# One more unit of seven products in each down-projection, its sums of weights made and split during the up-projection

## The chip, the cores and the metric

The kernel runs on one core of a Trainium2 chip. The metric is the device time of one execution in microseconds (us). The engines are named as the profile names them: PE multiplies matrices, DVE and ACT work on vectors, POOL is a slower vector engine, SP issues the large transfers.

## The reference, cut to what matters

A trunk of two decoder layers for 256 tokens of 1024 features, in float32. Each layer is an attention and a feed-forward; a final RMSNorm closes. With 256 tokens, layer 0's block-sparse attention is plain causal attention over 16 heads. Layer 1 is sliding-window attention (window 128, 4 shared key/value heads, a learned sink for each head). The feed-forward is what the change touches:

```python
def conv_ffn(h, w_up, conv_w, conv_b, w_down):
    S_ = h.shape[1]
    u = h @ w_up
    up = jnp.pad(u, ((0, 0), (CONV_W - 1, 0), (0, 0)))
    u = conv_b + sum(conv_w[j] * up[:, j:j + S_] for j in range(CONV_W))
    gate, val = jnp.split(u, 2, axis=-1)
    return (jax.nn.silu(gate) * val) @ w_down
...
    x = x + conv_ffn(rmsnorm(x, ffn_norm[l]), w_up[l], conv_w[l], conv_b[l], w_down[l])
```

`w_up` is 1024 x 5632 (2816 gate and 2816 value columns), `w_down` is 2816 x 1024, the convolution has width 3.

## The kernel before, in words

**Three products for one.** Every matrix product is made of three passes of PE in a reduced float32 format. Each operand is split into a hi part (the value rounded to that format) and a lo part (value minus hi); PE adds hi x hi, hi x lo and lo x hi. For weights, ACT makes the hi part (L216, `hi_part`, tile `wh`) and DVE the lo part (L227, `lo_part`, tile `wl`). So each weight costs PE time, an ACT pass and a DVE pass.

**Units.** Weights come in units of 128 x 2048 float32 (1 MB), fetched by SP (`fetch`, L180) into three raw buffers (`wr`), in the order in which they are used, and split into rings of four `wh` and four `wl` buffers. `prepare(i)` plans the fetching and splitting of unit i, and is called by `used(i - 4)` when the unit four before it has been put on PE. Steps are queued by `chain(key, (delay, function), ...)` against a planned clock that `tick` moves on with each matmul; `require(key)` issues what is left of a chain at once, because its result is now needed. `w_time` is the planned time of the next split: 4500 ns behind the last, 2500 behind a unit of sums.

**The order of the work.** Python's order of issue is the order on PE, ACT, DVE and SP until attention A starts; from there (`manual.close()`) a scheduler orders the instructions of each engine from that program. Within an engine instructions run in their order, so one that waits holds up all behind it.

**Feed-forward** (`ffn`, L771). First the up-projection: 22 units, each giving 128 gate and 128 value columns with 48 matmuls of 256 tokens. `post` (L810) does the convolution (ACT L827, DVE L831 and L833), the gate (ACT L837) and the product of gate and value (POOL L838, tile `m` or `q`). The result is hidden block i; two blocks make hidden pair i, the input of down unit i. For a normal down unit each block's hi part comes from ACT (L846) and its lo part from DVE (L847). These values live in `qd`, a ring of 15 buffers called quads (tile `q`), each of 128 x 1024.

Then the down-projection, class `Down`: 11 units, each 256 rows of `w_down`, added up in four PSUM banks `acc` (two blocks of tokens by two halves of the columns). A normal unit takes 8 products of 128 x 128 by 128 x 512, times three passes: 24 matmuls (L641, L642, L644).

**Units of seven.** A unit can do the same 2 x 2 block product with 7 products instead of 8, if sums and differences of blocks are made on both sides (`seventh`, L650; matmuls L668 to L670): 21 matmuls. The table `SEVEN` names them: units 3, 5 and 7 in layer 0; 3, 5, 7 and 8 in layer 1. What is added on the weights' side: four sums of 128 x 512 (`sums_of`, L193; DVE L199 makes two, L203 one each) in two quads, and their split, as a unit of its own of the `wh`/`wl` rings (a unit of sums, name `wl<-sums,wh`). The unit itself then needs only three of its four column blocks. On the side of the activations: four differences by POOL (`mix`, L854), then a hi part by ACT (L862) and a lo part by DVE (L866) of the whole 128 x 1024 pair (`split`, L856), in two quads; the raw quad is then free. Four products of each unit of seven go to extra PSUM banks, which `gather` (L675) adds at the end.

**Around it.** `v_sb` holds the values of attention A, and later, in the same tiles, those of attention B and a mask `near` for it, made by POOL behind attention A (L1109 to L1113). `kd` are two tiles of keys with zeros in their off-diagonal blocks (L944), used in the scores of both attentions.

## Time and profile before

| | |
|---|---|
| median of 3 runs | 542.82 us (542.77 to 543.08) |
| profiled execution | 542.62 us, span 540.9 us |
| granted clock of PE | 0.997 |
| moved by DMA | 100.99 MB, 187 GB/s over the span |

The span is the time from the first to the last instruction that the profile shows; 1.7 us of the profiled execution lie around it. All times in the views count from the span's start. In the timeline a row has a start, a length, the engine, the line, what is written and read, and how many instructions the row joins; in brackets stands the idle time ahead of it and what ended it. Instructions of an engine overlap a little in these rows (a matmul of 512 columns is shown as 0.38 us, while the next starts 0.22 behind it), so the distance between starts is the pace. Up-projection 0 runs to about 230.5 us and its down-projection to 285; in layer 1 to about 480 and 534.5.

### The profile page before, as it was taken

The numbers are of one execution on the slowest core, as the hardware profiler recorded it, in microseconds if no ns is written. First come the engines' busy times: TensorE is split into PE (matmuls) and PEld (weight loads), VectorE is DVE, ScalarE is ACT, GpSimd is POOL, SyncE is SP. The second block draws the span as 40 slices with busy tenths as digits, with TensorE's granted clock in tenths as the row PEclk, the third lists the DMA queues.
The fourth block names the chain that finished last, engine by engine and source line by source line (L and its number), as shares of the span: only waits on it lengthen the run. The fifth ranks groups of instructions, "written<-read, shape, count | busy, mean of one in ns | idle before, by whom it ended". The sixth has DMA issues, their size and how long they took to land.

```text
span 540.9 us, 9984 instructions
## 1 busy us (share of the span) xinstructions
PE 533.2 (99%) x3721; PEld 490.2 (91%) x3721; DVE 460.9 (85%) x911; ACT 385.7 (71%) x741; POOL 155.5 (29%) x196
## 2 busy tenths in 40 slices
PE   9999999999999999999999999999999999999995
PEld 7888888899999999988888887789999999998884
DVE  6798868689888978899889788889899789799995
ACT  6989776679566776656568798787657766676744
POOL 8322002011424434251010166202434344420004
PEclk9999999999999999999999999999999999999998
DMA  8974545342456656644664544233466466654502
GB/s 315 399 261 170 194 156 167 147 146 90 156 233 234 224 179 221 234 156 157 233 233 164 225 156 156 80 125 110 157 237 228 170 223 234 231 197 157 202 33 78
DMA packets 16608, 100.99 MB, mean 187 GB/s; under 512 B 1968, under 2 KB 2352, under 8 KB 6064
## 3 DMA queue, kind: packets, MB, share of 16 engines
q1 hardware_dynamic: 16272, 100.22, 51.3%
q8 instruction: 29, 0.48, 0.4%
q10 hardware_dynamic: 288, 0.13, 0.1%
q14 instruction: 19, 0.16, 0.1%
HBM read 99.30 MB, written 1.05 MB: 186 GB/s over the span
## 4 chain that ended last, share of the span: by engine, by line
PE 92%; ACT 4%; DVE 3%; issue 1%; POOL 0%; DVEq 0%; ACTq 0%
PE u L791 7%; PE u L792 7%; PE u L790 7%; PE acc L644 6%; PE acc L641 6%; PE acc L642 6%; PE t L792 6%; PE t L790 6%; PE t L791 6%; PE acc L399 5%; PE acc L401 5%; PE acc L400 5%; ACT m L522 2%; PE acc L933 2%; PE acc L792 2%; PE acc L791 2%
## 5 line engine op out<-in xcount | busy, mean ns | idle before, releaser
L227 DVE TENSOR_TENSOR wl<-wr,wh 128x1024 fp32r<-128x1024 f32 (+1 forms) x186 | 200.3, 1093 | 20.2 <-ACT wh L216 19.8
L216 ACT ACTIVATE wh<-wr 128x1024 fp32r<-128x1024 f32 (+1 forms) x190 | 174.0, 942 | 25.0 <-PE acc L644 8.1
L790 PE MATMUL u<-q,wh 128*128 128x256 f32 x320 | 88.3, 277 | 0.0
L791 PE MATMUL u<-q,wh 128*128 128x256 f32 x320 | 88.2, 276 | 0.1
L792 PE MATMUL u<-q,wl 128*128 128x256 f32 x320 | 87.9, 275 | 0.0
L838 POOL TENSOR_TENSOR m<-m,m 128x256 f32<-128x256 f32 x30 | 50.0, 1667 | 113.3 <-DVE m L833 66.0
L790 PE MATMUL t<-q,wh 128*128 128x256 f32 x288 | 79.2, 275 | 0.0
L791 PE MATMUL t<-q,wh 128*128 128x256 f32 x288 | 79.2, 275 | 0.0
L792 PE MATMUL t<-q,wl 128*128 128x256 f32 x288 | 79.2, 275 | 0.0
L641 PE MATMUL acc<-wh,q 128*128 128x512 f32 x182 | 71.0, 390 | 0.2 <-ACT q L599 0.2
L642 PE MATMUL acc<-wl,q 128*128 128x512 f32 x182 | 69.4, 381 | 0.0
L791 PEld LDWEIGHTS u<-q,wh 128*128 128x128 f32 x320 | 61.4, 192 | 0.3 <-DVE q L363 0.3
L792 PEld LDWEIGHTS u<-q,wl 128*128 128x128 f32 x320 | 61.4, 192 | 0.0
L790 PEld LDWEIGHTS u<-q,wh 128*128 128x128 f32 x320 | 61.3, 192 | 0.0
L644 PE MATMUL acc<-wh,q 128*128 128x512 f32 x182 | 58.2, 381 | 0.0
L790 PEld LDWEIGHTS t<-q,wh 128*128 128x128 f32 x288 | 55.3, 192 | 0.0
L791 PEld LDWEIGHTS t<-q,wh 128*128 128x128 f32 x288 | 55.3, 192 | 0.0
L792 PEld LDWEIGHTS t<-q,wl 128*128 128x128 f32 x288 | 55.3, 192 | 0.0
L399 PE MATMUL acc<-wh,q 128*128 128x512 f32 x128 | 50.0, 391 | 0.0
L400 PE MATMUL acc<-wl,q 128*128 128x512 f32 x128 | 48.8, 381 | 0.0
L401 PE MATMUL acc<-wh,q 128*128 128x512 f32 x128 | 48.6, 380 | 0.0
L641 PEld LDWEIGHTS acc<-wh,q 128*128 128x128 f32 x182 | 34.4, 189 | 5.5 <-ACT q L599 0.6
(218 smaller groups left out, 1174.1 us busy)
## 6 DMA issues: line engine op xcount, KB each, us to landing
wr<-in_w SPq DMA_DIRECT2D x82, 1024.0 KB, 4.8
wr<-in_w SPq DMA_DIRECT2D x16, 512.0 KB, 6.4
first<-in_xw SPq DMA_DIRECT2D x7, 384.0 KB, 6.4
xr<-in_x SPq DMA_DIRECT2D x2, 512.0 KB, 8.3
fin_t<-in_fin SPq DMA_DIRECT2D x1, 512.0 KB, 6.5
out<-ot SPq DMA_DIRECT2D x1, 512.0 KB, 2.6
first<-in_xw SPq DMA_DIRECT2D x1, 388.0 KB, 3.5
out<-yo SPq DMA_DIRECT2D x1, 256.0 KB, 2.1
```

Of the source, the lines that this page charges most:

```text
L216: nc.scalar.activation(wq[i][0][:, c], raw_of(i, c), AF.Copy, **({} if g is None else {"scale": g}))
L227: nc.vector.tensor_tensor(out=lo, in0=raw, in1=hi, op=ALU.subtract)
L399: nc.tensor.matmul(o, xh[:, blk(b)], wh, start=(c == 0), stop=False)
L400: nc.tensor.matmul(o, xh[:, blk(b)], wl, start=False, stop=False)
L401: nc.tensor.matmul(o, xl[:, blk(b)], wh, start=False, stop=(c == KC - 1))
L641: nc.tensor.matmul(o, ph[:, blk(b)], turns(hi[:, s_]), start=first, stop=False)
L642: nc.tensor.matmul(o, ph[:, blk(b)], turns(lo[:, s_]), start=False, stop=False)
L644: nc.tensor.matmul(o, pl[:, blk(b)], turns(hi[:, s_]), start=False, stop=end)
L790: nc.tensor.matmul(o, hi[:, s_], xh, start=(c == 0), stop=False)
L791: nc.tensor.matmul(o, hi[:, s_], xl, start=False, stop=False)
L792: nc.tensor.matmul(o, lo[:, s_], xh, start=False, stop=(c == KC - 1))
L838: nc.gpsimd.tensor_tensor(out=h, in0=gs, in1=t[1], op=ALU.mult)
```

## The change

Down unit 4 becomes a unit of seven too, in both layers (`SEVEN`). Its sums of weights (`MADE`) aren't made in the down-projection and take no place in the rings of `wh` and `wl`:

- A copy of unit 4's weights is fetched once more, into the raw ring ahead of up unit 12 (`AHEAD`). While the up-projection runs, `make` forms the four sums in place with four DVE additions of 128 x 512 (L231 of the new file) and splits them: hi by ACT (L234) into two tiles `made` that use the memory of `v_sb`, lo by DVE (L237) into the two `kd` tiles. The raw buffer is handed on to the next fetch only after that. `w_time` is moved by 4500 ns for it.
- In the down-projection unit 4 is fetched and split in three of its four blocks (`SHORT`: 1536 columns, split in 1024 and 512). `seventh` takes its sums from `made` and `kd`.
- Its hidden pair is handled like the other pairs of seven: product on POOL, `mix`, then `split` with a start 3500 ns ahead of its base time instead of 6500.
- In layer 0, `again` runs 4000 ns (planned) after unit 4: it allocates `v_sb` once more, makes `near` (which no longer happens behind attention A) and writes the zeros of `kd` by two ACT instructions of 128 x 1024. In layer 1 it isn't needed.

PE has 3 matmuls fewer in each layer.

```diff
@@ -51,25 +51,32 @@
-SEVEN = ((3, 5, 7), (3, 5, 7, 8))
-U_KV = U_DN0 + NF // 2 + len(SEVEN[0])
+SEVEN = ((3, 4, 5, 7), (3, 4, 5, 7, 8))
+MADE = (4, 4)
+RING = tuple(tuple(k for k in SEVEN[l_] if k != MADE[l_]) for l_ in range(2))
+U_KV = U_DN0 + NF // 2 + len(RING[0])
 U_QB = U_KV + 2
 U_OB = U_QB + 4
 U_UP1 = U_OB + 4
 U_DN1 = U_UP1 + NF
-N_UNITS = U_DN1 + NF // 2 + len(SEVEN[1])
+N_UNITS = U_DN1 + NF // 2 + len(RING[1])
 def slot(layer, i):
-    return (U_DN0, U_DN1)[layer] + i + sum(k < i for k in SEVEN[layer])
-SUMS = [slot(l_, i_) + 1 for l_ in range(2) for i_ in SEVEN[l_]]
-RAW = {}
+    return (U_DN0, U_DN1)[layer] + i + sum(k < i for k in RING[layer])
+SUMS = [slot(l_, i_) + 1 for l_ in range(2) for i_ in RING[l_]]
+SHORT = [slot(l_, MADE[l_]) for l_ in range(2)]
+AHEAD = 12
+RAW, WIDX = {}, {}
 for k_ in range(N_UNITS):
+    for l_ in range(2):
+        if k_ == (U_UP0, U_UP1)[l_] + AHEAD:
+            RAW["made", l_] = len(RAW)
     if k_ not in SUMS:
-        RAW[k_] = len(RAW)
-NEXT = {k_: min((j_ for j_ in RAW if RAW[j_] == n_ + 3), default=N_UNITS) for k_, n_ in RAW.items()}
+        RAW[k_], WIDX[k_] = len(RAW), len(WIDX)
+NEXT = {k_: next((j_ for j_ in RAW if RAW[j_] == n_ + 3), None) for k_, n_ in RAW.items()}
@@ -178,10 +185,12 @@
     def fetch(i):
-        if i < N_UNITS and i not in SUMS:
-            raws[i] = wp.tile([P, UNIT], F32, tag="raw", name=f"wr{i}", bufs=3)
-            for c in (slice(0, UNIT // 2), slice(UNIT // 2, UNIT)) if 2 <= i < 10 else (slice(0, UNIT),):
-                nc.sync.dma_start(raws[i][:, c], w[RAW[i]][:, c])
+        if i in RAW:
+            of = SHORT[i[1]] if isinstance(i, tuple) else i
+            raws[i] = wp.tile([P, UNIT], F32, tag="raw", name=nm("wr"), bufs=3)
+            for c in ((slice(0, UNIT // 2), slice(UNIT // 2, UNIT)) if 2 <= of < 10 else
+                      (slice(0, 3 * UNIT // 4 if i in SHORT else UNIT),)):
+                nc.sync.dma_start(raws[i][:, c], w[WIDX[of]][:, c])
@@ -203,6 +212,33 @@
         chain(("t", i), (500.0, both), (900.0, lambda: more(2, 0, 2)), (600.0, lambda: more(3, 2, 1)))
+    made_hi = []
+    def made_parts(k, part):
+        at = (0, 3, 2, 1)[k]
+        return (made_hi, made_lo)[part][at // 2][:, half(at % 2)]
+    def make(layer):
+        key = ("made", layer)
+        made_hi[:] = [one.tile([P, D], F32R, tag=f"v{b}", name=nm("made")) for b in range(NB)]
+        raw = raws[key]
+        s_ = [raw[:, half(k)] for k in range(4)]
+        def add(to, a, b):
+            nc.vector.tensor_tensor(out=s_[to], in0=s_[a], in1=s_[b], op=ALU.add)
+        def hi(n):
+            nc.scalar.activation(made_hi[n], raw[:, n * D:(n + 1) * D], AF.Copy)
+        def lo(n):
+            nc.vector.tensor_tensor(out=made_lo[n], in0=raw[:, n * D:(n + 1) * D], in1=f(made_hi[n]), op=ALU.subtract)
+        chain(key, (600.0, lambda: add(0, 0, 3)), (600.0, lambda: add(3, 2, 3)), (600.0, lambda: add(2, 0, 2)),
+              (600.0, lambda: add(1, 2, 1)), (600.0, lambda: hi(0)), (1000.0, lambda: hi(1)), (200.0, lambda: lo(0)),
+              (1000.0, lambda: lo(1)), (100.0, lambda: fetch(NEXT[key])))
@@ -260,8 +296,12 @@
                 sums_of(i + 2)
-        if i + 1 in SUMS:
+            for l_ in range(2):
+                if i + 1 == (U_UP0, U_UP1)[l_] + AHEAD:
+                    w_time[0] += 4500.0
+                    make(l_)
+        if i + 1 in SUMS or i in SHORT:
             cut[1] = slice(UNIT // 2, 3 * UNIT // 4)
...
@@ -650,25 +689,32 @@
             u = self.at(i)
+            made = i == MADE[self.layer]
             need(u)
-            need(u + 1)
+            if made:
+                require("made", self.layer)
+            else:
+                need(u + 1)
             self.wait(i)
             if not self.more:
                 self.more = [bank(t) for t in ("u", "t", "u", "t")]
             one, five, six, sev = self.more
-            (rh, rl), (th, tl) = wq[u], wq[u + 1]
+            def right(k, sum_, part):
+                return made_parts(k, part) if sum_ and made else wq[u + sum_][part][:, half(k)]
             xh, xl = self.parts[2 * i]
             (a00, a01), (a10, _) = self.acc
             own = dict(start=i == SEVEN[self.layer][0], stop=i == SEVEN[self.layer][-1])
-            for o, x_, hi, lo, k, mine in ((one, 0, rh, rl, 0, True), (six, 6, th, tl, 2, True), (five, 5, th, tl, 0, True),
-                                           (sev, 4, th, tl, 1, True), (a00, 2, rh, rl, 1, False), (a01, 7, rh, rl, 2, False),
-                                           (a10, 3, th, tl, 3, False)):
-                o, wh, wl = pairs(o), turns(hi[:, half(k)]), turns(lo[:, half(k)])
+            for o, x_, sum_, k, mine in ((one, 0, 0, 0, True), (six, 6, 1, 2, True), (five, 5, 1, 0, True), (sev, 4, 1, 1, True),
+                                         (a00, 2, 0, 1, False), (a01, 7, 0, 2, False), (a10, 3, 1, 3, False)):
+                o, wh, wl = pairs(o), turns(right(k, sum_, 0)), turns(right(k, sum_, 1))
                 c = blk(x_)
                 nc.tensor.matmul(o, xh[:, c], wh, start=mine and own["start"], stop=False)
                 nc.tensor.matmul(o, xh[:, c], wl, start=False, stop=False)
                 nc.tensor.matmul(o, xl[:, c], wh, start=False, stop=mine and own["stop"])
                 tick(3 * 512 / 2.4)
+            if made and self.layer == 0:
+                chain(("again",), (4000.0, again))
             if own["stop"]:
@@ -693,7 +739,8 @@
                     used(self.at(i))
-                    used(self.at(i) + 1)
+                    if i != MADE[self.layer]:
+                        used(self.at(i) + 1)
                     yield 21 * 512 / 2.4
@@ -862,7 +909,7 @@
             parts[2 * i] = tuple(t.rearrange("p c t -> p (c t)") for t in (hi, lo))
-            chain(("a", i), (5000.0 * (i - 2) + (300.0 if i == 3 else -6500.0), high),
+            chain(("a", i), (5000.0 * (i - 2) + (300.0 if i == 3 else -3500.0 if i == 4 else -6500.0), high),
                   (800.0, lambda: nc.vector.tensor_tensor(out=lo, in0=raw, in1=f(hi), op=ALU.subtract)))
...
@@ -1106,11 +1154,19 @@
-    near = v_sb[0][:, NKV:NKV + 4].rearrange("p h d -> p (h d)").rearrange("p (k t) -> p k t", k=2)
-    nc.gpsimd.memset(near, 1.0)
-    for k, (op, sign) in enumerate(((ALU.is_gt, 1), (ALU.is_ge, -1))):
-        nc.gpsimd.affine_select(out=near[:, k], in_=near[:, k], compare_op=op, fill=0.0, base=0,
-                                pattern=[[-sign, P]], channel_multiplier=sign)
+    near = []
+    def again():
+        v_sb[:] = [one.tile([P, NH, HD], F32, tag=f"v{b}", name=nm("v")) for b in range(NB)]
+        near.append(v_sb[0][:, NKV:NKV + 4].rearrange("p h d -> p (h d)").rearrange("p (k t) -> p k t", k=2))
+        nc.gpsimd.memset(near[0], 1.0)
+        for k, (op, sign) in enumerate(((ALU.is_gt, 1), (ALU.is_ge, -1))):
+            nc.gpsimd.affine_select(out=near[0][:, k], in_=near[0][:, k], compare_op=op, fill=0.0, base=0,
+                                    pattern=[[-sign, P]], channel_multiplier=sign)
+        for t in kd:
+            nc.scalar.activation(t.rearrange("p a b t -> p (a b t)").rearrange("p (k t) -> p k t", t=P),
+                                 ones.unsqueeze(1).to_broadcast([P, 8, P]), AF.Copy, scale=0.0)
...
```

Where the order of instructions moves, three places (rows are line, operation, output, inputs, shape; the numbers in the names of tiles tell buffers apart and differ between the two programs).

The first is the start of layer 0's down-projection, on DVE. Before: lo part of pair 3, first half of unit 3's sums, a block's lo part (L847), lo part of pair 5, second half of unit 3's sums, a block's lo part.

```order
L866 TENSOR_TENSOR q_3000<-q_1854,q_2999 128x1024
L227 TENSOR_TENSOR wl_3059<-sums_2989,wh_3058 128x1024
L847 TENSOR_TENSOR q_2853<-m_284_2924,q_2853 128x256
L866 TENSOR_TENSOR q_3002<-q_2142,q_3001 128x1024
L227 TENSOR_TENSOR wl_3059<-sums_2990,wh_3058 128x1024
L847 TENSOR_TENSOR q_2853<-m_291_2998,q_2853 128x256
```

The same place now (L913 is the lo part of a pair, L263 of weights, L894 of a block); the L913 rows are pairs 3, 4 and 5.

```order
L913 TENSOR_TENSOR q_3007<-q_1851,q_3006 128x1024
L263 TENSOR_TENSOR wl_3068<-sums_2996,wh_3067 128x1024
L894 TENSOR_TENSOR q_2860<-m_328_2931,q_2860 128x256
L913 TENSOR_TENSOR q_3009<-q_1993,q_3008 128x1024
L263 TENSOR_TENSOR wl_3068<-sums_2997,wh_3067 128x1024
L913 TENSOR_TENSOR q_3011<-q_2141,q_3010 128x1024
L894 TENSOR_TENSOR q_2860<-m_336_3005,q_2860 128x256
```

The lo part of pair 4 has the place that pair 5 had, and pair 5 comes behind the second half of unit 3's sums.

On ACT at the same place, before: hi parts of unit 3's sums, with that of pair 5 (L862) between them, then of a block (L846) and of unit 4's weights.

```order
L216 ACTIVATE wh_3058<-sums_2989 128x1024
L862 ACTIVATE q_3001<-q_2142 128x1024
L216 ACTIVATE wh_3058<-sums_2990 128x1024
L846 ACTIVATE q_2853<-m_291_2998 128x256
L216 ACTIVATE wh_3093<-wr_2910 128x1024 x2
```

And now (L909 is the hi part of a pair, L893 of a block, L252 of weights):

```order
L252 ACTIVATE wh_3067<-sums_2996 128x1024
L252 ACTIVATE wh_3067<-sums_2997 128x1024
L893 ACTIVATE q_2860<-m_336_3005 128x256
L909 ACTIVATE q_3010<-q_2141 128x1024
L252 ACTIVATE wh_3104<-wr_2917 128x1024
L252 ACTIVATE wh_3104<-wr_2917 128x512
L909 ACTIVATE q_3012<-q_2430 128x1024
```

The hi part of pair 5 now stands behind that of the block, which reads what POOL's product wrote; the one of pair 4 went ahead of these rows.

The second place is layer 1's down-projection on DVE, between units 3 and 6. Before: pairs 5, 7 and 8 are the L866 rows, with the sums of unit 5 (L199, L203) and the weights of units 4 and 5 between them.

```order
L866 TENSOR_TENSOR q_6003<-q_5144,q_6002 128x1024
L847 TENSOR_TENSOR q_5853<-m_569_5998,q_5853 128x256
L199 TENSOR_TENSOR sums_6134<-wr_5981 128x1024
L227 TENSOR_TENSOR wl_6097<-wr_5910,wh_6096 128x1024 x2
L203 TENSOR_TENSOR sums_6135<-sums_6134,wr_5981 128x512
L203 TENSOR_TENSOR sums_6135<-sums_6135,wr_5981 128x512
L866 TENSOR_TENSOR q_6005<-q_5428,q_6004 128x1024
L227 TENSOR_TENSOR wl_6131<-wr_5981,wh_6130 128x1024
L227 TENSOR_TENSOR wl_6131<-wr_5981,wh_6130 128x512
L866 TENSOR_TENSOR q_6007<-q_5569,q_6006 128x1024
L227 TENSOR_TENSOR wl_6171<-sums_6134,wh_6170 128x1024
```

Now the L913 rows are pairs 5 and 7; pair 8 follows three rows below the last one.

```order
L913 TENSOR_TENSOR q_6030<-q_5161,q_6029 128x1024
L263 TENSOR_TENSOR wl_6126<-wr_5935,wh_6125 128x1024
L263 TENSOR_TENSOR wl_6126<-wr_5935,wh_6125 128x512
L208 TENSOR_TENSOR sums_6163<-wr_6006 128x1024
L212 TENSOR_TENSOR sums_6164<-sums_6163,wr_6006 128x512
L212 TENSOR_TENSOR sums_6164<-sums_6164,wr_6006 128x512
L263 TENSOR_TENSOR wl_6160<-wr_6006,wh_6159 128x1024
L263 TENSOR_TENSOR wl_6160<-wr_6006,wh_6159 128x512
L913 TENSOR_TENSOR q_6032<-q_5450,q_6031 128x1024
L263 TENSOR_TENSOR wl_6197<-sums_6163,wh_6196 128x1024
```

Unit 4's lo part is shorter by half a row, the sums of unit 5 come after it and not around it, and pair 7 stands behind the weights of unit 5.

The third place is a little later in layer 1, on DVE: the sums of unit 8 and their lo parts. Before:

```order
L227 TENSOR_TENSOR wl_6249<-sums_6223,wh_6248 128x1024
L199 TENSOR_TENSOR sums_6275<-wr_6162 128x1024
L227 TENSOR_TENSOR wl_6268<-wr_6162,wh_6267 128x512
L203 TENSOR_TENSOR sums_6276<-sums_6275,wr_6162 128x512
L203 TENSOR_TENSOR sums_6276<-sums_6276,wr_6162 128x512
L227 TENSOR_TENSOR wl_6302<-sums_6275,wh_6301 128x1024
L227 TENSOR_TENSOR wl_6302<-sums_6276,wh_6301 128x1024
```

And now (L208 and L212 are the additions, L263 the lo parts):

```order
L263 TENSOR_TENSOR wl_6284<-sums_6249,wh_6283 128x1024
L208 TENSOR_TENSOR sums_6301<-wr_6191 128x1024
L263 TENSOR_TENSOR wl_6299<-wr_6191,wh_6298 128x512
L212 TENSOR_TENSOR sums_6302<-sums_6301,wr_6191 128x512
L263 TENSOR_TENSOR wl_6328<-sums_6301,wh_6327 128x1024
L212 TENSOR_TENSOR sums_6302<-sums_6302,wr_6191 128x512
L263 TENSOR_TENSOR wl_6328<-sums_6302,wh_6327 128x1024
```

The last addition stood ahead of both lo parts; now it stands between them.

More of the change, by code (lines that the diff above doesn't have):

```diff
@@ L320, in trunk @@
     for b in range(NB):
-        t = one.tile([P, NH, HD], F32, name=f"v{b}")
-        v_sb.append(t)
+        v_sb.append(one.tile([P, NH, HD], F32, tag=f"v{b}", name=nm("v")))
     def warm_up(n):
@@ L553, in part @@
                 nc.vector.tensor_tensor(out=pT[:, :, 1:], in0=tp[:, :, 1:].to_broadcast(shape),
-                                        in1=near.unsqueeze(1).to_broadcast(shape), op=ALU.mult)
+                                        in1=near[0].unsqueeze(1).to_broadcast(shape), op=ALU.mult)
             chain(("pT", j), (200.0, lambda: nc.scalar.activation(pT[:, :, 0], tp[:, :, 0], AF.Copy)), (100.0, part))
@@ L946, in trunk @@
         nc.gpsimd.memset(f(t), 0.0)
+    made_lo = [t.rearrange("p a b t -> p (a b t)") for t in kd]
     invf = rb[:, 144:152]
@@ L1298, in pack @@
     rows2(inp["w_down"][1], SEVEN[1])
-    assert len(units) == len(RAW)
+    assert len(units) == len(WIDX)
     wpk = np.stack(units)
```

## The prediction

> **What bounds the kernel.** I read the head of the page first: busy time by engine, as a share of the span.
>
> ```profile
> span 540.9 us, 9984 instructions
> PE 533.2 (99%) x3721; PEld 490.2 (91%) x3721; DVE 460.9 (85%) x911; ACT 385.7 (71%) x741; POOL 155.5 (29%) x196
> ```
>
> The matmuls fill 99% of the span. The waits of PE show whether anything holds it up now (engine, line, what it waited for, total, times, longest):
>
> ```profile
> PE u L329 <- DVE warm L304: 1.1, 1, 1.1
> PE u L547 <- ACT m L532: 0.2, 1, 0.2
> PE acc L641 <- ACT q L599: 0.2, 1, 0.2
> ```
>
> No wait of PE lies in a feed-forward. A matmul taken out is time taken out, as long as its operands still come in time. Who makes them is the next question: the windows of the two down-projections (busy time of each engine with its count, then the granted clock, the DMA share and GB/s).
>
> ```profile
> core 0: us, PE busy (x) PEld busy (x) DVE busy (x) ACT busy (x) POOL busy (x), PEclk, DMA share, GB/s
> 230.50:284.50 54.00, 54.00 (x257) 47.09 (x255) 49.22 (x65) 33.13 (x47) 12.71 (x12) 1.00 0.53 195
> 480.40:534.50 54.10, 54.10 (x257) 47.50 (x257) 50.25 (x63) 34.09 (x46) 8.97 (x6) 1.00 0.35 127
> ```
>
> PE is full, but DVE, which makes the lo parts and the sums, is at 49.2 and 50.3 of 54 us. The change takes work from PE in this stage and must not bring DVE's results later. So the case is decided by the lead of each split over its first matmul there.
>
> **The gain.** PE's timeline around unit 3 (seven products) and unit 4 (eight) of layer 0 (start, length, line, output and inputs):
>
> ```profile
> 246.11 0.38 PE L668 MATMUL u<-wh,q 128*128 128x512 f32 x1
> ...
> 250.43 0.38 PE L670 MATMUL acc<-wh,q 128*128 128x512 f32 x1
> 250.64 0.38 PE L641 MATMUL acc<-wh,q 128*128 128x512 f32 x1
> ```
>
> The 21 matmuls of the seven take 250.64 - 246.11 = 4.53 us, 0.2157 each from start to start (the 0.38 overlap). A normal unit has 24, 5.18 us. Unit 4 thus saves 3 x 0.2157 = 0.65 us in each layer, 1.29 us at most.
>
> **The work that is added.** The durations, grouped by line and form (busy, mean ns):
>
> ```profile
> L227 DVE TENSOR_TENSOR wl<-wr,wh 128x1024 fp32r<-128x1024 f32 x135 | 167.0, 1246 | 14.3 <-ACT wh L216 14.2
> L216 ACT ACTIVATE wh<-wr 128x1024 fp32r<-128x1024 f32 x139 | 144.6, 1055 | 20.7 <-PE acc L644 6.4 <-issue 3.9 <-PE t L791 3.4
> L838 POOL TENSOR_TENSOR m<-m,m 128x256 f32<-128x256 f32 x30 | 50.0, 1667 | 113.3 <-DVE m L833 66.0 <-ACT m L837 27.6 <-ACT m L827 11.3
> L854 POOL TENSOR_TENSOR q<-q 128x128 f32<-128x128 f32 x28 | 20.9, 747 | 2.2
> wr<-in_w SPq DMA_DIRECT2D x82, 1024.0 KB, 4.8
> ```
>
> These lengths overlap too; back to back, DVE puts a 128x1024 subtraction 1.135 us behind the one before and a 128x512 one 0.60 (starts in the layer 1 fence below: 502.85 to 503.98, 508.52 to 509.12).
>
> In the middle of each up-projection the change adds to DVE four additions of 128x512 and two lo parts of 128x1024: 4 x 0.60 + 2 x 1.135 = 4.7 us; to ACT two hi parts, some 2 us; to SP one transfer of 1 MB (4.8 us to land); to POOL four mixes of 0.75. It takes from DVE there the two lo parts of hidden pair 4, which are these, with the idle time before them:
>
> ```profile
> 172.04 0.43 DVE L847 TENSOR_TENSOR q<-m,q 128x256 fp32r<-128x256 f32 x1 [1.64 <-ACT q L846]
> ...
> 179.26 0.42 DVE L847 TENSOR_TENSOR q<-m,q 128x256 fp32r<-128x256 f32 x1 [0.68 <-ACT q L846]
> 179.60 0.48 DVE L833 SCALAR_TENSOR_TENSOR m<-u,cp,m 128x254 f32<-128x254 f32 x1
> 179.99 0.48 DVE L831 SCALAR_TENSOR_TENSOR m<-u,cp,m 128x255 f32<-128x255 f32 x1
> 180.38 1.22 DVE L227 TENSOR_TENSOR wl<-wr,wh 128x1024 fp32r<-128x1024 f32 x1
> ```
>
> That returns 2.3 us of idle and 0.7 of work, so DVE comes out some 1.7 us later. The last row ends the lo part of up unit 14, at 181.60; PE uses it first here:
>
> ```profile
> 187.91 0.28 PE L792 MATMUL u<-q,wl 128*128 128x256 f32 x1
> ```
>
> A lead of 6.3 us against 1.7 for DVE. The raw ring is the tighter part: the copy takes one of its three buffers, so unit 14 is fetched after the made sums are split instead of before, and 4.8 us of transfer stand in that lead. I cost the stage at nothing, with 0 to 1 us as bounds: below nothing is excluded, since PE waits for nothing there; above 1 the lead would have to be gone altogether. The rebuilding of the mask and zeros behind unit 4 of layer 0 adds two ACT instructions, about 1.9 us at that row's pace, to a queue that has 1.97 us free at that place:
>
> ```profile
> 256.07 1.58 ACT L216 ACTIVATE wh<-wr 128x1024 fp32r<-128x1024 f32 x2 [1.97 <-issue]
> ```
>
> Nothing again, with PE 4 us away; without that cover, a weight part 1.9 us later, inside the leads of 4 to 5 us that ordinary units have here.
>
> **Down-projection of layer 0.** On DVE unit 4 gives up a 512 column lo part (0.60) and takes on the lo part of its activations (1.135): +0.54 in all, and more in the order. DVE, then POOL, then ACT, in before:
>
> ```profile
> 239.78 1.21 DVE L866 TENSOR_TENSOR q<-q,q 128x1024 fp32r<-128x1024 f32 x1
> 240.92 1.21 DVE L227 TENSOR_TENSOR wl<-sums,wh 128x1024 fp32r<-128x1024 f32 x1
> 243.20 0.43 DVE L847 TENSOR_TENSOR q<-m,q 128x256 fp32r<-128x256 f32 x1 [1.07 <-ACT q L846]
> ```
>
> ```profile
> 237.43 5.29 POOL L838 TENSOR_TENSOR m<-m,m 128x256 f32<-128x256 f32 x1 [4.62 <-ACT wh L216]
> ```
>
> ```profile
> 242.75 0.42 ACT L846 ACTIVATE q<-m 128x256 fp32r<-128x256 f32 x1 [3.52 <-POOL m L838]
> ```
>
> The activations of pair 5 were split at 239.78. Now pair 4 has that place, and ACT's hi part of pair 5 stands behind the hi part that waits for POOL, so it runs from 243.07 to 244.0. DVE goes on at 244.1: pair 5 (1.135), h (0.34), first sum (1.135), unit 4 (1.135 + 0.60), two sums (1.20), pair 7 (1.135), unit 5 (1.735), half of its sums (1.135), half of unit 6 (1.135), and the second half of unit 5's sums from 254.8 to 256.0. PE needs that at its fifth matmul of unit 5: 250.64 + 4.53 + 4 x 0.2157 = 256.03. The cover is used up exactly: 0.05 us of wait, between 0 (everything 0.3 earlier) and 0.6 (half an instruction later). **Layer 0: -0.65 + 0.05 = -0.60.**
>
> POOL's 5.29 us, against a mean of 1.67, lie under DVE's unbroken run of subtractions and end 0.7 us after DVE went idle. [...]
>
> **Down-projection of layer 1.** Pair 4 now keeps a hi and a lo buffer where it kept one, so the ring of quads frees a place one step later. In before DVE met that at pair 8; in the order of after it meets it at pair 7. DVE in before:
>
> ```profile
> 500.57 1.23 DVE L866 TENSOR_TENSOR q<-q,q 128x1024 fp32r<-128x1024 f32 x1 [0.42 <-PE acc L669]
> 501.71 1.22 DVE L227 TENSOR_TENSOR wl<-sums,wh 128x1024 fp32r<-128x1024 f32 x1
> 502.85 1.22 DVE L227 TENSOR_TENSOR wl<-wr,wh 128x1024 fp32r<-128x1024 f32 x1
> 503.98 1.22 DVE L227 TENSOR_TENSOR wl<-sums,wh 128x1024 fp32r<-128x1024 f32 x1
> ...
> 508.52 0.69 DVE L203 TENSOR_TENSOR sums<-sums,wr 128x512 f32<-128x512 f32 x1
> 509.12 0.68 DVE L227 TENSOR_TENSOR wl<-wr,wh 128x512 fp32r<-128x512 f32 x1
> ...
> 516.07 1.41 DVE L203 TENSOR_TENSOR sums<-sums,wr 128x512 f32<-128x512 f32 x2
> 517.39 2.43 DVE L227 TENSOR_TENSOR wl<-sums,wh 128x1024 fp32r<-128x1024 f32 x2
> ```
>
> ```profile
> 500.51 0.38 PE L641 MATMUL acc<-wh,q 128*128 128x512 f32 x1
> ...
> 520.80 0.38 PE L669 MATMUL u<-wl,q 128*128 128x512 f32 x1
> ```
>
> The release is unit 3's last product, just before PE's first row (unit 4 begins). So DVE starts at 500.57 as before, but with pair 7 and pair 8 still to do: one 1.135 more. From 500.57 to the last sums of unit 8 stand 12 instructions of 1.135 and 5 of 0.60, 16.6 us: 517.2. Then the order itself is worse: half the lo part of unit 8's sums (to 518.3), the third sum (518.95), ACT's hi part that needs it (0.1 to start and 0.95, to 520.05), and the last lo part from 520.1 to 521.3. In before both sums stood ahead of both lo parts, which ended at 519.8. PE wants it at 520.80 - 0.65 = 520.15: late by 1.15 us. I take that; it is 0 if the release comes a subtraction earlier, and 1.8 if another half subtraction stands ahead. Units 5 and 7 keep 0.7 us by the same count (505.2 for 505.9, 514.9 for 515.6). What follows moves with PE. **Layer 1: -0.65 + 1.15 = +0.50.**
>
> **Sum.** -0.60 + 0.50 = -0.1. The profiled execution took 542.62 us (540.9 of span and 1.7 around it), so it would take 542.5; it lies 0.2 below the median of the runs, 542.82, and from that the forecast is **542.7 us**. What a measurement of this kernel can tell from no change is about 0.2%, 1.1 us; the forecast is no change, with its own range 542.0 to 543.6 (0.7 better if layer 1's cover half holds, 0.9 worse at the upper ends of both waits).
>
> **Rivals.** *Clean gain.* The last lo part of unit 8's sums comes in time and both layers keep 0.65: 542.82 - 1.29 = 541.5. For it: the two waits are small differences of long counts, and 7% in DVE's pace would close the larger, 1.15 of 16.6 us. Against it: DVE has under 4 us of idle in 54, and the sum, hi part and lo part of unit 8 now follow one another whatever the pace. Chance 0.13.
>
> *Slower, by POOL in layer 0.* POOL's multiplication at 237.43 ends only when DVE goes idle. If DVE has one subtraction and one h more before that idle time (1.135 + 0.34), ACT's hi parts of h and pair 5 come 1.5 us later, and unit 5's sums with them: layer 0 -0.65 + 1.5 = +0.85, with layer 1 +1.35, 544.2 us. It decides from a delay of about 1.2 us. For it: the 5.29 us, and no slack behind it. Against it: the same number of DVE instructions lies there as before. Chance 0.14.
>
> *The up-projection starves.* The transfer of unit 14 or the made sums come so late that PE waits there. The lead of 6.3 less 4.8 of transfer and 1.7 of DVE is close to zero only if they add up in a row, while the transfer starts under DVE's work; 1 us in each layer, with the -0.1 of above, would give 544.7. Chance 0.04.
>
> *The saving isn't there*: the seven's matmuls might take longer than a normal unit's. The 4.53 us for 21 rule it out.
>
> Forecast 0.69 (all of it within 0.2%). Faster by over 0.2% 0.13, within 0.2% 0.69, slower 0.18. The range reaches to the clean gain below and to 544.0 above, which leaves most of the slower cases out.
>
> **What would show it.** PE's waits in the profile of after should name DVE's lo part of sums at the seventh products, about 1.1 us in unit 8 of layer 1 and next to none elsewhere. DVE's pair 7 in layer 1 should start behind PE's last product of unit 3, and between the two halves of unit 8's sums DVE should idle about 1.1 us for ACT. In layer 0 pair 5's lo part should start near 244.1. The up-projections should show no wait of PE. It is wrong if PE's waits in the down-projections sum to under 0.2 us, or over 2.4, or if any stands in an up-projection.

## The result, and the profile after

The changed kernel takes 545.74 us (median of 7 runs, 544.94 to 548.70) against 542.82 us: a ratio of 1.007, with a 95% interval of 1.004 to 1.010. It is slower by 2.9 us, where no change was forecast and 544.0 was the upper end. The profiled execution took 545.69 us. The experiments below were run beside the kernel before, which took 542.94 us there (1 to 4), 542.73 (5 to 7), 543.20 (8 to 11) and 542.91 (12 and 13); three runs with a granted clock of 0.95 or less (554.2 and 927.84 us of the kernel before, 613.85 of the made work alone) are left out of the ratios. From the page of the changed kernel:

```profile
span 544.0 us, 10019 instructions
PE 532.9 (98%) x3715; PEld 488.8 (90%) x3715; DVE 471.1 (87%) x921; ACT 389.6 (72%) x745; POOL 170.1 (31%) x204
```

PE has its six matmuls fewer; DVE is busy 10.2 us longer. The waits of PE that are new, from its timeline:

```profile
258.35 0.48 PE L713 MATMUL u<-wl,q 128*128 128x512 f32 x1 [2.27 <-DVE wl L263]
522.55 0.48 PE L712 MATMUL u<-wh,q 128*128 128x512 f32 x1 [0.41 <-ACT wh L252]
523.81 0.48 PE L713 MATMUL u<-wl,q 128*128 128x512 f32 x1 [0.78 <-DVE wl L263]
```

The brackets count the time in which PE is empty. From start to start, against the usual 0.22, the wait in layer 0 costs 2.44 us, those in layer 1 0.57 and 1.04. The first is at unit 5 of layer 0, the others at unit 8 of layer 1: the two places of the prediction, but 2.44 where it had 0.05 and 1.61 where it had 1.15.

A table by stage, from PE's timelines, helps for all that follows. The times count from start to start: from the first to the last matmul of an up-projection, from there to the first of the key/value projection (287.1 us in before; in layer 1 to PE's last matmul), and between. The kernel before in us, the others as differences from it:

| kernel | up 0 | down 0 | middle | up 1 | down 1 |
|---|---|---|---|---|---|
| before | 118.83 | 56.64 | 74.29 | 118.94 | 54.43 |
| changed | 0 | +1.94 | +0.25 | 0 | +1.07 |
| changed, two more profiles (a, b) | 0 | +1.38, +1.38 | +0.25, +0.23 | 0 | +0.83, +1.31 |
| layer 0 only | 0 | +3.86 | +0.26 | 0 | 0 |
| layer 1 only | 0 | 0 | 0 | 0 | +0.83 |
| no additions | 0 | -0.49 | +0.24 | 0 | +0.83 |
| pair 5 first | 0 | +2.33 | +0.24 | 0 | +0.83 |
| layer 1, sums first | 0 | 0 | 0 | 0 | -0.26 |
| additions on POOL | +0.82 | +5.93 | +0.24 | +0.64 | +0.99 |
| sums in the ring | 0 | +2.77 | 0 | 0 | +1.50 |
| made at unit 17 | 0 | +4.09 | +0.23 | 0 | +1.44 |
| made at unit 8 | +1.74 | +0.68 | +0.24 | +1.23 | +0.83 |
| made work alone | 0 | +3.41 | 0 | 0 | +1.27 |

The up-projections, where the work was added, are as long as before. Both down-projections are longer, although each has 0.65 us less to multiply. The row of the changed kernel sums to 3.3 us, and the start before up-projection 0 was 0.1 shorter, which makes the 3.1 by which the span has grown.

The 0.25 in the middle stands at one place, the third of four transposes behind the first key/value matmuls. PE in before and in the changed kernel, then DVE in both:

```profile
289.04 0.60 PE L342 MATMUL t<-ident,xr 128*128 128x128 f32 x4
```

```profile
290.85 0.85 PE L381 MATMUL t<-ident,xr 128*128 128x128 f32 x4
```

```profile
288.25 0.41 DVE L352 TENSOR_TENSOR q<-t,q 128x256 fp32r<-128x256 f32 x1
```

```profile
289.73 0.74 DVE L265 SCALAR_TENSOR_TENSOR wl<-wr,cp,wh 128x512 fp32r<-128x512 f32 x1
290.39 0.42 DVE L811 TENSOR_TENSOR xr<-acc,xr 128x256 f32<-128x256 f32 x1
290.73 0.42 DVE L391 TENSOR_TENSOR q<-t,q 128x256 fp32r<-128x256 f32 x1
```

In before DVE has read the transposes ahead of these (tile `t`) 0.4 us before PE's row starts. In the changed kernel a weight part (L265) stands between the two additions to `xr`, the reading ends at 291.15, and the third transpose starts at 291.29. In the made work alone DVE has the order of before there, and the 0.25 are absent.

Why unit 5 is late is read back through rows of the changed kernel. DVE first (L913 is a pair's lo part: 3, 4, 5), with pair 3 of the kernel before ahead of them, then POOL and ACT:

```profile
237.18 1.21 DVE L866 TENSOR_TENSOR q<-q,q 128x1024 fp32r<-128x1024 f32 x1
```

```profile
239.10 1.21 DVE L913 TENSOR_TENSOR q<-q,q 128x1024 fp32r<-128x1024 f32 x1
...
241.71 1.21 DVE L913 TENSOR_TENSOR q<-q,q 128x1024 fp32r<-128x1024 f32 x1
...
246.07 1.23 DVE L913 TENSOR_TENSOR q<-q,q 128x1024 fp32r<-128x1024 f32 x1 [2.02 <-ACT q L909]
...
256.99 1.30 DVE L263 TENSOR_TENSOR wl<-sums,wh 128x1024 fp32r<-128x1024 f32 x1
```

```profile
239.35 5.30 POOL L885 TENSOR_TENSOR m<-m,m 128x256 f32<-128x256 f32 x1 [4.62 <-ACT wh L252]
```

```profile
244.68 0.42 ACT L893 ACTIVATE q<-m 128x256 fp32r<-128x256 f32 x1 [4.47 <-POOL m L885]
```

Everything stands as the prediction had it, one thing excepted: it stands 1.9 us later. Pair 3 starts at 239.10, in before at 237.18; POOL's product at 239.35 for 237.43, as long as before; ACT's hi part at 244.68 for 242.75. Pair 5 starts at 246.07 where 244.1 was forecast, and the second half of unit 5's sums at 256.99 for 254.8. DVE entered the down-projection late.

How it came to that shows in DVE's convolution steps. The start of the first one of block 21, the last of up-projection 0, in before and in the changed kernel:

```profile
234.41 0.47 DVE L831 SCALAR_TENSOR_TENSOR m<-t,cp,m 128x255 f32<-128x255 f32 x1
```

```profile
236.33 0.47 DVE L878 SCALAR_TENSOR_TENSOR m<-t,cp,m 128x255 f32<-128x255 f32 x1
```

The same step of other blocks, read in the same way, as differences from before: block 6 -0.9, block 8 +3.3, block 11 +0.8, block 13 -0.2, block 14 +3.1, block 17 +2.1, block 21 +1.9. DVE is made late at blocks 7 and 8, where the made work stands on it (161.49 to 172.56 us); up to block 14 the difference swings, since DVE's steps stand in another order there, and then it stays near 2. PE meanwhile lives on the leads of the weights, of which 2 to 3 us are left at the least, and waits for nothing. In before, DVE's start of the last block lies 3.7 us behind the end of that block's matmuls; DVE isn't waiting for PE there, it has a backlog, and what is added to it is still there when the down-projection begins. It isn't full: in before it is busy for 102.9 of the 118.9 us of up-projection 0, and 15.6 of the rest are waits for ACT. In three profiles of the changed kernel no engine waits for a transfer of weights in up-projection 0.

### The profile page after: what moved, and what is told of

Its sections match the earlier page's. It is cut to its first block, busy times and chain, and to the rows that moved or that the text cites. A ratio compares the mean times of both kernels' runs of the same rounds, so it can differ in the third digit from the quotient of the medians.

```text
span 544.0 us, 10019 instructions
## 1 busy us (share of the span) xinstructions
PE 532.9 (98%) x3715; PEld 488.8 (90%) x3715; DVE 471.1 (87%) x921; ACT 389.6 (72%) x745; POOL 170.1 (31%) x204
## 4 chain that ended last, share of the span: by engine, by line
PE 68%; DVE 16%; ACT 6%; issue 4%; POOL 4%; DVEq 0%; POOLq 0%; ACTq 0%
DVE wl L263 7%; PE u L838 5%; PE u L839 5%; PE u L837 5%; PE acc L438 5%; PE acc L440 5%; PE acc L439 5%; PE t L837 4%; PE t L839 4%; PE t L838 4%; PE acc L683 3%; PE acc L680 3%; PE acc L681 3%; POOL m L885 2%; ACT wh L252 2%
## 5 line engine op out<-in xcount | busy, mean ns | idle before, releaser
L263 DVE TENSOR_TENSOR wl<-wr,wh 128x1024 fp32r<-128x1024 f32 (+1 forms) x186 | 199.6, 1089 | 14.6 <-ACT wh L252 14.3
L252 ACT ACTIVATE wh<-wr 128x1024 fp32r<-128x1024 f32 (+1 forms) x190 | 172.6, 936 | 11.0 <-PE acc L683 3.9
L885 POOL TENSOR_TENSOR m<-m,m 128x256 f32<-128x256 f32 x26 | 46.7, 1796 | 97.5 <-DVE m L880 49.1
L680 PE MATMUL acc<-wh,q 128*128 128x512 f32 x166 | 64.9, 391 | 0.2 <-ACT q L638 0.2
L681 PE MATMUL acc<-wl,q 128*128 128x512 f32 x166 | 63.4, 382 | 0.0
L683 PE MATMUL acc<-wh,q 128*128 128x512 f32 x166 | 53.5, 381 | 0.0
L438 PE MATMUL acc<-wh,q 128*128 128x512 f32 x128 | 50.0, 391 | 0.0
L439 PE MATMUL acc<-wl,q 128*128 128x512 f32 x128 | 48.8, 381 | 0.0
L440 PE MATMUL acc<-wh,q 128*128 128x512 f32 x128 | 48.6, 380 | 0.0
L885 POOL TENSOR_TENSOR q<-m,m 128x256 f32<-128x256 f32 x18 | 28.2, 1566 | 41.7 <-DVE m L880 16.0
```

The costliest lines, as they stand in the source:

```text
L252: nc.scalar.activation(wq[i][0][:, c], raw_of(i, c), AF.Copy, **({} if g is None else {"scale": g}))
L263: nc.vector.tensor_tensor(out=lo, in0=raw, in1=hi, op=ALU.subtract)
L438: nc.tensor.matmul(o, xh[:, blk(b)], wh, start=(c == 0), stop=False)
L439: nc.tensor.matmul(o, xh[:, blk(b)], wl, start=False, stop=False)
L440: nc.tensor.matmul(o, xl[:, blk(b)], wh, start=False, stop=(c == KC - 1))
L680: nc.tensor.matmul(o, ph[:, blk(b)], turns(hi[:, s_]), start=first, stop=False)
```

## The experiments

**1. Layer 0 only**

```diff
-SEVEN = ((3, 4, 5, 7), (3, 4, 5, 7, 8))
-MADE = (4, 4)
+SEVEN = ((3, 4, 5, 7), (3, 5, 7, 8))
+MADE = (4, None)
...
```

> The change in layer 0 alone; layer 1 has its units of seven as before. The trace of the changed kernel shows PE waiting 2.44 us at the second product of unit 5 in layer 0, and 0.38 us more than before at the transposes behind that down-projection. If the two layers don't act on each other, this kernel keeps those and loses 0.65: 542.8 - 0.65 + 2.8 = 545.0 us. If part of layer 1's loss came from the lateness of layer 0, it stays near 545.0 here and layer 1 alone comes out clean. Rival, that layer 0's wait is an accident of one execution: within 0.5 us of 542.8.

Measured: 545.74 us (6 runs, 544.11 to 547.38; before 542.94), ratio 1.005 (1.003 to 1.007). The wait at unit 5 is there, 2.68 us from start to start. The runs lie in two groups, 544.11 to 544.82 and 546.65 to 547.38, as those of the changed kernel do (544.94 to 545.74 and 548.39 to 548.70). The profiled execution, 547.38, is one of the upper group. PE behind the wait:

```profile
259.33 0.62 PE L713 MATMUL u<-wl,q 128*128 128x512 f32 x1 [2.52 <-DVE wl L263]
259.74 0.63 PE L714 MATMUL u<-wh,q 128*128 128x512 f32 x1
...
262.30 0.63 PE L714 MATMUL t<-wh,q 128*128 128x512 f32 x1
262.73 0.50 PE L712 MATMUL acc<-wh,q 128*128 128x512 f32 x1
263.06 0.38 PE L713 MATMUL acc<-wl,q 128*128 128x512 f32 x1
```

And the windows around it, with the granted clock as the third number from the end:

```profile
250.00:256.00 6.00, 6.00 (x29) 5.25 (x28) 5.96 (x8) 5.76 (x7) 0.00 (x0) 1.00 0.49 175
256.00:260.00 4.00, 1.48 (x6) 0.97 (x5) 4.00 (x4) 2.52 (x3) 2.12 (x3) 0.94 0.81 262
260.00:263.00 3.00, 3.00 (x8) 2.37 (x8) 3.00 (x4) 0.00 (x0) 0.00 (x0) 0.51 0.45 137
263.00:270.00 7.00, 7.00 (x34) 6.11 (x34) 6.01 (x7) 3.91 (x4) 0.00 (x0) 1.00 0.68 245
```

Behind the wait the matmuls start 0.43 us apart instead of 0.22, for 3.4 us; the granted clock is 0.51 from 260 to 263 us. The wait cost 2.68 us and the slow stretch behind it 1.8. So the loss in layer 0 stands by itself, and in this execution it has a second part.

**2. Layer 1 only**

```diff
-SEVEN = ((3, 4, 5, 7), (3, 4, 5, 7, 8))
-MADE = (4, 4)
+SEVEN = ((3, 5, 7), (3, 4, 5, 7, 8))
+MADE = (None, 4)
...
```

> The change in layer 1 alone. The trace of the changed kernel shows 1.61 us of waits at unit 8 of layer 1 (0.57 for ACT's hi part, 1.04 for DVE's lo part). If the layers don't act on each other: 542.8 - 0.65 + 1.6 = 543.8 us. If layer 1 has a wait only because layer 0 came late: 542.2 us. The runs of the changed kernel lie in two groups, near 545.3 and near 548.5; the layer that causes the upper group shows it here or in the run of layer 0 alone.

Measured: 543.71 us (11 runs, 543.41 to 544.10), ratio 1.0016 (1.0007 to 1.0024). The waits at unit 8 are 1.37 us, and nothing like an upper group appears. The layers' losses add up; layer 0 has the larger one and the spread.

**3. The additions left out**

```diff
-        chain(key, (600.0, lambda: add(0, 0, 3)), (600.0, lambda: add(3, 2, 3)), (600.0, lambda: add(2, 0, 2)),
-              (600.0, lambda: add(1, 2, 1)), (600.0, lambda: hi(0)), ...
+        chain(key, (3000.0, lambda: hi(0)), ...
```

> The four DVE additions that make the sums in each up-projection are left out, so the copy of unit 4 itself is split and multiplied in place of the sums; all else stands. Theory of the carry (the work put into the up-projection makes DVE later, and DVE stays later until the down-projection, since it never idles long enough): DVE has 2.4 us less in each layer, pair 3 of layer 0 is split about 2 us earlier, the wait of 2.44 us in layer 0 goes, that of layer 1 falls by 0.3 to 0.6 only, since its order of sums stays: 542.8 to 543.1 us. Theory of the order alone (pair 5's hi part behind the one that waits for POOL): layer 0 keeps at least 1.5 us of its wait, 544.6 us. Theory of the transfer (the third fetch into the raw ring): no change from the changed kernel, 545.7.

Measured: 543.53 us (11 runs, 543.22 to 543.86), ratio 1.0010 (1.0001 to 1.0019). The waits of PE that are left:

```profile
PE u L712 <- DVE wl L262: 0.8, 1, 0.8
...
PE u L711 <- ACT wh L251: 0.2, 1, 0.2
```

Both are at unit 8 of layer 1. In layer 0 there is none, DVE reaches block 21 at 234.48 (0.07 behind before), and down-projection 0 is 0.49 us shorter than before: the gain that was forecast. Pair 5's hi part still stands behind the one that waits for POOL. 2.4 us of DVE work, taken out of the middle of the up-projection, decide over the wait some 90 us later; this is the carry. The order of layer 0's down-projection is the same here on every engine, so it alone doesn't make the wait. The transfer isn't the same (the raw buffer is free at 164.76 instead of 172.56); against it speaks that no engine waits for a transfer in up-projection 0 of the changed kernel. The time is 0.4 to 0.7 above what was expected, part of it in the middle (+0.24).

**4. Pair 5 first**

```diff
-            ... -3500.0 if i == 4 else -6500.0), high),
+            ... -3500.0 if i == 4 else -9500.0 if i == 5 and layer == 0 else -6500.0), high),
```

> In layer 0 the hi part of pair 5 is planned 3000 ns earlier, so on ACT it stands ahead of the block's hi part that waits for POOL, and on DVE ahead of pair 4; all work is done. Theory of the order: the 2.02 us that DVE idles ahead of pair 5's lo part shrink by the 1.1 us of that instruction or more, and the wait at unit 5 from 2.44 to between 0.4 and 1.3: 543.7 to 544.6 us. Theory of the carry: the same upper end, 544.6, because the block's lo part still waits for POOL's late product. Theory of the transfer: no change, 545.7.

Measured: 545.37 us (5 runs, 544.00 to 546.05), ratio 1.004 (1.003 to 1.005). Both theories expected less. The profiled execution is the slowest of the five. In it the idle time of 2.02 us ahead of pair 5 is gone, but the second half of unit 5's sums still comes at 257.59 and the wait is 2.84 us: DVE was 1.9 us later still when it entered the down-projection (the first addition for unit 3 at 234.83, for 232.91 in the changed kernel). 1.1 of these came up in the middle of the up-projection, where ACT waited for a transfer and DVE for ACT; the changed kernel has neither wait in its profiles:

```profile
183.74 1.08 ACT L252 ACTIVATE wh<-wr 128x1024 fp32r<-128x1024 f32 x1 [1.34 <-DMA wr<-in_w]
```

```profile
184.85 1.23 DVE L263 TENSOR_TENSOR wl<-wr,wh 128x1024 fp32r<-128x1024 f32 x1 [1.05 <-ACT wh L252]
```

From that first addition to unit 5's sums it is 22.76 us here and 24.08 in the changed kernel. So the order is worth 1.3 us (its theory had 1.1 or more), and the lateness took them back: the wait in layer 0 has both causes, a chain without cover and a late start of it, and in this execution the transfer made the start later.

**5. Layer 1 only, with unit 8's sums first**

The first half of the lo part is made to follow the third addition; beside experiment 2, only these two instructions change places on DVE.

```diff
...
-            with tc.issue_after(copies[1].ins) if i == U_QK[3] and c.start else ExitStack():
+            after = copies[1] if i == U_QK[3] and c.start else last_sum[i] if i == SUMS[-1] else None
+            with tc.issue_after(after.ins) if after is not None else ExitStack():
...
```

> The change in layer 1 alone, and the third addition of unit 8's sums put ahead of the first half of their lo part again, as it stood before; nothing else moves. Theory of the order in layer 1: DVE's idle of 1.12 us for ACT's hi part goes, PE's 1.37 us of waits at unit 8 (measured with layer 1 alone, 543.7 us) fall to about 0.25, 542.6 us. Theory of the carry alone (DVE simply has too much work, in whatever order): the last lo part ends as late as before, waits of at least 1 us, 543.5 us or more.

Measured: 542.82 us (11 runs, 542.40 to 543.31) beside 542.73, ratio 0.9999 (0.9991 to 1.0008). DVE with layer 1 only (experiment 2), then with the sums first:

```profile
517.92 1.23 DVE L263 TENSOR_TENSOR wl<-sums,wh 128x1024 fp32r<-128x1024 f32 x1
519.07 0.69 DVE L212 TENSOR_TENSOR sums<-sums,wr 128x512 f32<-128x512 f32 x1
520.87 1.23 DVE L263 TENSOR_TENSOR wl<-sums,wh 128x1024 fp32r<-128x1024 f32 x1 [1.12 <-ACT wh L252]
```

```profile
516.64 1.41 DVE L214 TENSOR_TENSOR sums<-sums,wr 128x512 f32<-128x512 f32 x2
517.98 2.43 DVE L266 TENSOR_TENSOR wl<-sums,wh 128x1024 fp32r<-128x1024 f32 x2
```

The idle 1.12 us are gone, PE waits 0.27 instead of 1.37, and the stage is 0.26 us shorter than before. In layer 1 it was the order. It is the best version found, and it only equals the kernel before: what it gains in its stage is too small to be seen in the time.

**6. The additions on POOL (and unit 8's sums first)**

```diff
-            nc.vector.tensor_tensor(out=s_[to], in0=s_[a], in1=s_[b], op=ALU.add)
+            nc.gpsimd.tensor_tensor(out=s_[to], in0=s_[a], in1=s_[b], op=ALU.add)
...
```

> The changed kernel in both layers with two edits: the four additions that make the sums in each up-projection run on POOL instead of DVE (all work is done), and the order of unit 8's sums as in the run before this one. Theory of the carry: DVE is relieved of the same 2.4 us as when the additions were left out, which took away the wait in layer 0, and layer 1 keeps 0.25: 542.8 - 1.3 + 0.4 + 0.3 = 542.2 us. Rival, that POOL and DVE hold each other up when both take two operands from SBUF: POOL's additions, 1.3 us each when alone, stretch to several times that under DVE's subtractions or stop DVE, the gate products behind them come late and with them the hi parts for which DVE waits: a wait of 1 us or more in layer 0, 543.5 us or more.

Measured: 551.68 us (5 runs, 550.49 to 552.51), ratio 1.016 (1.014 to 1.017). POOL's four additions, and DVE at that time:

```profile
160.97 6.21 POOL L233 TENSOR_TENSOR wr<-wr 128x512 f32<-128x512 f32 x4 [2.28 <-DMA wr<-in_w]
```

```profile
161.20 2.12 DVE L266 TENSOR_TENSOR wl<-wr,wh 128x1024 fp32r<-128x1024 f32 x1
...
166.94 1.33 DVE L239 TENSOR_TENSOR kd<-wr,made 128x1024 fp32r<-128x1024 f32 x1 [3.22 <-ACT made L236]
```

The time is the rival's, the larger cause isn't. The additions take 1.55 us each, where POOL's subtractions of this size (L262, eight of them in this run) take 1.29, and DVE's subtraction beside them 2.12 for 1.21: the two do hold each other up, by about 1 us. But 3.22 us are lost because the made sums' lo part stands in DVE's queue at the place where DVE's own additions would have been ready, and now waits for ACT, and that for POOL. DVE is 6.0 us late at block 21 (4.6 against PE, which waits in the up-projections too, 0.75 us in layer 0), and waits of 1.78 and 3.11 us follow in down-projection 0.

**7. Sums in the ring**

```diff
-SEVEN = ((3, 5, 7), (3, 5, 7, 8))
+SEVEN = ((3, 4, 5, 7), (3, 4, 5, 7, 8))
```

(to the kernel before, nothing else)

> The kernel before with unit 4 added to the table of sevens in both layers, so that its sums are made and split in the down-projection like those of the other units; no copy is fetched and nothing is made ahead. The matmuls saved are the same, 1.29 us. If only DVE's sum of work counted (4.6 us more in each layer, wherever it stands), this is like the changed kernel, 545 to 546 us. If the place counts, because of the 4.7 us put into the up-projection some 2.8 are absorbed there by idle time, waits of some 4 us in each layer and 549 us or more, with the clock lowered behind them.

Measured: 548.23 us (5 runs, 547.69 to 548.44), ratio 1.0096 (1.008 to 1.011). Between the two expectations: 2.77 us more in down-projection 0 and 1.50 in 1. The work made ahead, as the change does it, costs less than the same work in the down-projection; but it costs.

**8 and 13. The made work alone**

The table of sevens is that of before; the copy is still fetched, added and split, and unit 4 is a normal unit.

```diff
-SEVEN = ((3, 4, 5, 7), (3, 4, 5, 7, 8))
+SEVEN = ((3, 5, 7), (3, 5, 7, 8))
...
-RING = tuple(tuple(k for k in SEVEN[l_] if k != MADE[l_]) for l_ in range(2))
+RING = SEVEN
...
```

> The kernel before with only the work that was put into the up-projections: the copy of unit 4 is fetched, added up and split in the middle of each, and nothing uses the result; unit 4 stays a normal unit of 24 matmuls, and all that is computed stands as before. If the up-projection absorbs the work, as the prediction had it: 542.8 us, no change. Theory of the carry: DVE has 4.7 us more, comes 3 us or more later to the down-projection, and the sums of unit 5 in layer 0 (lead 1.91 us before) and of unit 8 in layer 1 (0.98, with 1.6 us of idle ahead of it) are late: waits of 1 to 3 us in layer 0 and 0 to 2 in layer 1, 544 to 548 us.

Measured: 547.58 us (6 runs, 546.28 to 549.21), ratio 1.0085 (1.007 to 1.010). Four of the six have a clock of 0.994 or 0.995. A second profile of this kernel:

> The kernel of the run with the made work alone once more, for a profile in which the clock isn't lowered throughout. It took 547.6 us, 4.4 more than the kernel before. Theory of the carry: no wait of PE in the up-projections, DVE's lo part of pair 3 in layer 0 3 us or more later than in the kernel before (237.2), waits of 2 to 4 us at unit 4 or 5 of layer 0 and up to 2 in layer 1. Rival: the waits lie in the up-projections, behind the transfer.

Measured: 547.90 (the profiled execution) and 547.05 us. PE's waits, and DVE at block 21:

```profile
PE u L713 <- DVE wl L263: 3.9, 3, 2.5
```

```profile
240.37 0.47 DVE L878 SCALAR_TENSOR_TENSOR m<-t,cp,m 128x255 f32<-128x255 f32 x1
```

PE waits for the made work in no up-projection. DVE comes 6.0 us late to block 21 of layer 0, 5.3 against PE, where 4.7 us of work were added. That is 3.3 more than in the changed kernel, which is spared pair 4's lo parts and the idle time at them; the prediction had 3.0 for these. In down-projection 0 PE then waits 0.52 and 2.69 us, in 1 1.16 us. So the work that the prediction put at nothing costs some 4.4 us (547.58 for 543.20) where pair 4 gives nothing back. It isn't the work of DVE alone: as nothing uses the made sums, the zeros of `kd` are written early too, by two ACT instructions in up-projection 0 (172.34 and 174.16 us), and their share isn't measured.

**9. Made at unit 17**, and **12. made at unit 8**

```diff
-AHEAD = 12
+AHEAD = 17
```

(and `AHEAD = 8` in experiment 12)

> The changed kernel with the copy fetched ahead of up unit 17 instead of 12, all else the same. Theory of the carry: DVE never makes up for the work, so where in the up-projection it stands makes no difference: 545 to 547 us, with a wait of 2 to 3 us in layer 0. Rival, that the wait comes from the transfers that crowd at unit 12 (leads of 5 to 7 us there, 8 to 10 at unit 17): the wait in layer 0 falls under 1 us, 543.5 us.

> The changed kernel with the copy fetched ahead of up unit 8 instead of 12. At unit 17 the same work cost 3 us more than at unit 12, so the place counts. Theory A, that DVE makes up for part of the work as the up-projection goes on: earlier is better, the wait in layer 0 falls under 1.5 us (2.4 at unit 12, 4.5 in two waits at unit 17) and the up-projection shows none or a small one, since its leads at unit 8 are 3 us: 543.5 to 545 us. Theory B, that unit 12 stands well only because the idle time that pair 4 frees lies there: waits as at unit 17 or in the up-projection, 546 us or more.

Measured: 548.99 us at unit 17 (4 runs, 548.03 to 549.38), ratio 1.011 (1.009 to 1.012); 548.18 at unit 8 (4 runs, 547.39 to 548.68), ratio 1.010 (1.008 to 1.012). The waits at unit 17, then at unit 8:

```profile
PE u L713 <- DVE wl L263: 4.9, 3, 2.9
```

```profile
PE t L839 <- DVE wl L263: 2.1, 2, 1.3
PE u L713 <- DVE wl L263: 1.8, 2, 1.0
```

At unit 17 DVE is 4.5 us late at block 21, and waits of 1.38 and 3.11 us stand in down-projection 0. That the place makes no difference was wrong; that the transfers crowd at unit 12 was wrong too. Most of the lateness at unit 17 comes up behind the made work (block 17 -0.1, block 18 +3.2), where DVE's order differs too; why is open. At unit 8 the wait in down-projection 0 is 1.17 us, under the 1.5 of theory A, but PE waits in the up-projection itself (1.46 from start to start in layer 0), where a unit's lo part stands behind the made ones on DVE (157.07 to 159.97 us) and ends at 162.62, while PE could have used it at 161.2. So the same work is paid for in either place, and unit 12 is the better compromise of the three.

**10 and 11. The changed kernel, two more profiles**

> The changed kernel once more, for its profile. Its runs lie near 545.3 or near 548.5 us. Theory of the clock: in a run of the upper group the matmuls behind the wait in layer 0 start 0.43 us apart instead of 0.22 for some 3.4 us, as they did behind the wait of 2.7 us in the run with layer 0 alone; in one of the lower group they don't. Rival: the upper group has a longer wait.

> The same kernel as in the look before this one, with the same expectation.

Both, 545.27 and 545.67 us, are of the lower group: a wait of 1.89 us at unit 5 and no slow matmul behind it. They fit the theory of the clock and can't test it alone. The clocks of all runs help: the seven of the changed kernel have a mean clock of 0.997 or 0.998 up to 545.74 us, and 0.993 to 0.996 from 548.39 up; with layer 0 only it is 0.998 or 0.999 up to 544.82, and 0.994 or 0.995 from 546.65 up.

## Why the prediction was wrong

- *The gain* was right: 0.65 us in each layer, seen nearly clean in layer 0 without the additions (-0.49; of the rest 0.11 stands at one matmul of unit 5, which starts 0.32 us behind the one before it for 0.22, and 0.04 at a transpose).
- *"I cost the stage at nothing, with 0 to 1 us as bounds"* is the step that failed. The same paragraph had DVE "some 1.7 us later", and this was nearly exact: 1.9 at the last block. What was wrong was to compare these 1.7 with the leads of the up-projection and then drop them. The chain of layer 0 was then worked out from the starts of before (pair 5's place at 239.78), as if DVE began the down-projection on time. With 1.9 added at its head, the same chain gives a wait of 2.0; 2.4 was measured; two subtractions at its end took 0.1 longer each (1.31 and 1.30 us long for 1.22), and PE came 0.1 early. Of the 3.2 us between the 542.5 that the prediction had for the profiled execution and its 545.69, this wait is 2.4, the one in layer 1 0.5 and the middle 0.25.
- DVE's lateness at block 21 against PE's last matmul of the up-projection, and the waits in down-projection 0, go together across the experiments with the change in layer 0: -0.2 and 0 without the additions, 0.9 and 1.2 at unit 8, 1.6 and 1.9 in both other profiles of the changed kernel, 2.0 and 2.4 in the first, 2.3 and 2.7 with layer 0 only, 4.2 and 4.5 at unit 17, 4.6 and 4.9 with the additions on POOL. Pair 5 first is the exception, 3.8 and 2.8, and there the chain behind was made 1.3 us shorter.
- *The down-projection of layer 0, "the cover is used up exactly"*, was right and should have been the warning: with a cover of zero, whatever is late upstream counts in full. The prediction's own sign of being wrong, waits of over 2.4 us in the down-projections, was met with 4.05.
- *The down-projection of layer 1* was right in mechanism and near in size: 1.15 forecast, 1.61, 1.36 and 1.84 measured in three profiles, ACT's hi part and the 1.12 us of DVE's idle at the place named. Turning the order back removed 1.1 of it. Pair 7 started at 502.86, 0.30 after PE's last product of unit 3, because DVE was late here too; that is part of the rest.
- *Not seen at all*: the lowered clock behind a long wait, and the 0.25 us in the middle of the program in every kernel that has the change in layer 0, which go with DVE's order there. Three of the seven runs of the changed kernel lie some 3 us above the others at a lower clock; 1.8 of such a difference are shown, by the profile of experiment 1, and the rest is open.
- *The rivals.* "Slower, by POOL in layer 0" had the right place, came nearer than the forecast with 544.2, and had the wrong cause: POOL's product was as long as before, and late because DVE's steps ahead of it were. "The up-projection starves" didn't happen at unit 12, and did at unit 8. In experiment 6 a subtraction of DVE's took 2.12 us beside POOL's additions, for 1.21 without. POOL's product in down-projection 0 of the changed kernel took 5.30 us, for 5.29 before, so its loss isn't explained by the two holding each other up.

## What to carry to other kernels

Idle time of an engine with a backlog need not be a free place: in before DVE idles for 16 of 119 us of up-projection 0, nearly all of it in waits for ACT; and where 4.7 us were added alone (experiment 13), 5.3 of lateness stood at the end of layer 0's up-projection, and 2.5 at that of layer 1's. Work put into a stage where nothing waits for it can still be ahead of whatever that engine does next, so carry the lateness over the stage's end and compare it with the smallest lead there. A stage in which PE doesn't wait says nothing of the engine behind it; look at how late that engine's steps are against the matmuls that feed them. And a scheduler's order near the end of a stage can be worth as much as the change itself (1.1 us here for one addition that slipped behind one subtraction).
